# Hybrid encoder on one core: natural token order, banded first dilated group, softmax statistics carried between orders

## The chip, the cores and the metric

The kernel runs on one core of one Trainium2 chip. The metric is device microseconds of one execution; lower is better. The engines are TensorE (PE: matmuls and transposes; its weight loads are listed apart as PEld), VectorE (DVE), ScalarE (ACT), GpSimd (POOL) and SyncE (SP, which here only issues DMAs).

## What is computed

Two layers, 512 tokens, model width 1024, 256 memory tokens. Every layer makes one normalised input, projects it, and runs three branches: differential attention (8 heads, two softmax maps each), dilated attention (3 groups of 4 heads with head width 128), and cross-attention into memory. Each branch is gated by a SiLU path, projected, weighed by sigmoid gates and merged. The change is in the dilated branch:

```python
DIL_GROUPS = ((128, 1), (512, 4), (2048, 16))          # (window, dilation)
for g, (window, dilation) in enumerate(DIL_GROUPS):
    o_g, lse_g = dilated_group(lq[:, :, g], lk[:, :, g], lv[:, :, g], window, dilation, bias_g)
wts = softmax(stack(lses), axis=0)                       # over the groups
o_b = einsum('gbsh,gbshe->bshe', wts, stack(outs))
```

A query of group 0 sees keys at a distance of at most 64 tokens; one of group 1 sees keys of its own class modulo 4 at a distance of at most 256; one of group 2 sees keys of its own class modulo 16. The groups are combined by their softmax denominators, so for a token one softmax over the union of the keys of all three groups gives the same result.

## The kernel before, in words

All large products are made from fp32 values split into a high and a low fp32r part; `mm3` (lines 214 to 217) issues three matmuls for a product. The normalised input lies transposed in `hT_hi` and `hT_lo` [128, 8, 512]. Lines 63 and 64 load and store tokens by class modulo 4: position 128*c + a holds token 4*a + c, so the four chunks of 128 positions are the four classes.

Weights stream in through `load` (line 171, SP queue) in an order written out by hand (`weight_order`), and are split by ScalarE (line 106) and VectorE (line 107) a few units ahead (`prefetch`). `proj_fm` makes 128 features of all tokens (24 matmuls of 512 columns); `proj_tm` makes up to 512 features token-major (four chunks, 96 matmuls as wide as the features).

The attention of a layer is four steps j. In each, `weave` interleaves the tracing of the projections of dilated head j (`dil_proj`) with differential heads 2j and 2j+1 (`diff_att`), and then the projections for the next differential heads (`diff_proj`) with the attention of dilated head j (`dil_att`). The scheduler of the framework then orders each engine's instructions by its own timeline; each engine executes them in that order.

`dil_att` (lines 610 to 660) goes over the four chunks c. For group 0 it makes the scores of 128 queries against all 512 keys (line 628); the bias tile holds minus 1e30 where the key is out of the window, because in class order the window is spread over all four chunks. For groups 1 and 2 it makes 128 x 128 scores within the class, in plain fp32 (line 631). One minimum over both (lines 632 and 635), one exponential over 768 columns (line 638), one reciprocal and one scaling (lines 639 and 640) give the weights of all three groups. They are transposed: four blocks for group 0 (helper, line 506), two for groups 1 and 2 (line 644). V of group 0 is applied with `mm3` to 256 queries at a time (line 650), V of groups 1 and 2 in plain fp32 (line 655), all accumulated in the PSUM tile `d_o`. `dil_proj` makes V of the three groups as one `proj_tm` of 384 features (line 607). `qk_keep` (line 586) copies Q and K of groups 1 and 2 out of PSUM.

`bias_tables` (line 325) makes the bias rows in layer 0 and stores them to DRAM on POOL's queue; `load_bias` (line 361) reads a tile of 7 pieces for a head. `right_sums` (line 256) makes sums of quarters of hT on VectorE (line 259) and stores them to `t_d` (line 281, SP queue) for the matrix products of `pair` in the later merge; it is traced in step j = 1. `diff_norm` (line 557) squares the differential outputs, sums over features with a matmul by ones (lines 565 and 566), and stores the result.

Of the kernel before, what the change touches and what calls it, by code (L numbers as in the profile page):

```python
# [9 lines left out]
F32 = mybir.dt.float32  # L10
F32R = mybir.dt.float32r
# [14 lines left out]
TW = 7 * 255  # L26
# [23 lines left out]
def dil_v_cols(h):  # L50
    return [(g * 128, (g + 1) * 128, LV + g * 512 + h * 128) for g in range(3)]
# [3 lines left out]
def encoder_kernel(ctx: ExitStack, tc: tile.TileContext, x, mem, g_norm, w_in, diff_lambda,  # L55
                   w_mem_kv, g_mem, w_br_diff, w_br_dil, w_br_mem, w_out, rel_bias, g_final,
                   buckets, maskrows, partrows, out):
# [5 lines left out]
    x_v = x[0].rearrange("(a c) d -> c a d", c=4)  # L63
    out_v = out[0].rearrange("(a c) d -> c a d", c=4)
# [23 lines left out]
    tt_d = dr.tile([12, 32, TW], F32, name="tt_d")  # L88
# [21 lines left out]
    def weight_order():  # L110
# [19 lines left out]
        for l in range(DEPTH):  # L130
# [123 lines left out]
    H0, H1 = slice(0, 256), slice(256, 512)  # L254

    def right_sums(pool):

        def acc(out, x, y, op):
            nc.vector.tensor_tensor(out=out, in0=x, in1=y, op=op)

        for k2 in range(2):
            def quarter(kh, ts):
                ks = slice(4 * kh + 2 * k2, 4 * kh + 2 * k2 + 2)
# [3 lines left out]
            t1, t2, t3, t4 = [pool.tile([128, 2, 256], F32, tag="ts", name="t_sum", bufs=4) for _ in range(4)]  # L267
# [12 lines left out]
            for i, t in enumerate((t1, t2, t3, t4)):  # L280
                dma(t_d[i, k2], t)
            yield
# [42 lines left out]
    def bias_tables(pool):  # L325
# [21 lines left out]
        for n0 in range(0, TW, 512):  # L347
            n = min(512, TW - n0)
# [4 lines left out]
            for r in range(4):  # L353
                v = t[r * N_BIAS:r * N_BIAS + 12, 0:n]
                pdma(tt_d[:, r * 8:(r + 1) * 8, n0:n0 + n], v[:, None, :].to_broadcast([12, 8, n]))
                if n0 == 512:
                    v = t[r * N_BIAS + 12:(r + 1) * N_BIAS, 253:508]
                    pdma(t0_d[:, r * 8:(r + 1) * 8, :], v[:, None, :].to_broadcast([8, 8, 255]))

    def load_bias(dst, h):  # L360

        b, nd, w = (tt_d[h], 7, TW) if h < 12 else (t0_d[h - 12], 1, 255)
        for a in range(0, 128, 32):
            dma(dst[a:a + 32], bass.AP(b.tensor, b.offset + 127 - a, [[w - 1, 32], [255, nd], [1, 128]]))
# [91 lines left out]
    def proj_tm(l, key, n, keep):  # L456
# [52 lines left out]
    def diff_att(l, j, P, proj, lam):  # L509
        Q, K, vhi, vlo = proj  # L510
        O = []
        for s in range(2):
            h = 2 * j + s
            bt = P["al"].tile([128, 7, 128], F32, tag="bt", name="f_bias", bufs=2)
# [3 lines left out]
            for half in range(2):  # L518
                whi = P["ae"].tile([128, 4, 256], F32R, tag="x4", name="f_wThi", bufs=4)
                wlo = P["ae"].tile([128, 4, 256], F32R, tag="x4", name="f_wTlo", bufs=4)  # L520
                for c2 in range(2):
# [4 lines left out]
                    for m in range(2):  # L526
                        sp = ps.tile([128, 4, 128], F32, tag="s", name="f_s", bufs=2)
# [4 lines left out]
                        nc.vector.tensor_tensor_reduce(  # L532
                            out=em.rearrange("p (c b) -> p c b", c=4), in0=sp, in1=bt[:, 3 - c:7 - c],
                            op0=ALU.add, op1=ALU.min, scale=-1.0, scalar=3e38, accum_out=stt[:, m:m + 1])
# [22 lines left out]
    def diff_norm(j, P, O):  # L557

        for s, o in enumerate(O):
# [3 lines left out]
            split(sqh, sql, sq)  # L563
            ms = mm([128, S], name="f_ms")
# [19 lines left out]
    def qk_keep(ae, o, scale, name):  # L584
        t = ae.tile([128, S], F32, tag="dqk", name=name, bufs=10)
        nc.scalar.activation(t, o, AF.Copy, scale=scale)
        return t

    def dil_proj(l, h, P):
# [9 lines left out]
        vhi = P["ae"].tile([128, 4, 128], F32R, tag="v1", name="d_vhi", bufs=2)  # L599
        vlo = P["ae"].tile([128, 4, 128], F32R, tag="v1", name="d_vlo", bufs=2)  # L600
        v23 = P["ae"].tile([128, 4, 256], F32, tag="v6", name="d_v23", bufs=2)

        def keep(c, o):
            split(vhi[:, c], vlo[:, c], o[:, 0:128])
            nc.scalar.activation(v23[:, c], o[:, 128:384], AF.Copy)

        yield from proj_tm(l, ("lv", h), 384, keep)
        return Q, K, vhi, vlo, v23

    def dil_att(l, h, P, proj):  # L610
        Q, K, vhi, vlo, v23 = proj
        bt = P["al"].tile([128, 7, 128], F32, tag="bt", name="d_b1", bufs=2)
        load_bias(bt, 8 + h)
        b2 = P["al"].tile([128, 2, 128], F32, tag="b2", name="d_b2", bufs=1)
        load_bias(b2[:, 0:1], 12 + h)
        load_bias(b2[:, 1:2], 16 + h)
        o = ps.tile([128, S], F32, tag="o", name="d_o", bufs=1)
        for half in range(2):
            whi = P["ae"].tile([128, 4, 256], F32R, tag="x4", name="d_wThi", bufs=4)
            wlo = P["ae"].tile([128, 4, 256], F32R, tag="x4", name="d_wTlo", bufs=4)  # L620
            w23 = P["al"].tile([128, 2, 256], F32, tag="w2", name="d_w23", bufs=2)
            for c2 in range(2):
                c = 2 * half + c2
                cs = slice(c * 128, (c + 1) * 128)
                stt = st.tile([128, 8], F32, tag="fst", name="d_st")
                e = P["al"].tile([128, 768], F32, tag="e3", name="d_e", bufs=2)
                sp = ps.tile([128, 4, 128], F32, tag="s", name="d_s1", bufs=2)
                mm3(sp, Q[0][0][:, cs], Q[0][1][:, cs], K[0][0], K[0][1], True, True)
                sp2 = ps.tile([128, 2, 128], F32, tag="s", name="d_s2", bufs=2)
                for g in (1, 2):  # L630
                    nc.tensor.matmul(sp2[:, g - 1], lhsT=Q[g][:, cs], rhs=K[g][:, cs], start=True, stop=True)  # L631
                nc.vector.tensor_tensor_reduce(
                    out=e[:, 0:512].rearrange("p (c b) -> p c b", c=4), in0=sp, in1=bt[:, 3 - c:7 - c],
                    op0=ALU.add, op1=ALU.min, scale=-1.0, scalar=3e38, accum_out=stt[:, 0:1])
                nc.vector.tensor_tensor_reduce(
                    out=e[:, 512:768].rearrange("p (c b) -> p c b", c=2), in0=sp2, in1=b2,
                    op0=ALU.add, op1=ALU.min, scale=-1.0, scalar=stt[:, 0:1], accum_out=stt[:, 1:2])
                nc.scalar.activation(e, e, AF.Exp, scale=-1.0, bias=stt[:, 1:2], accum_out=stt[:, 2:3])
                nc.vector.reciprocal(stt[:, 3:4], stt[:, 2:3])
                nc.vector.tensor_scalar(e, e, stt[:, 3:4], None, op0=ALU.mult)  # L640
                transposed(whi, wlo, [e[:, k * 128:(k + 1) * 128] for k in range(4)], c2 * 128)
                t = ps.tile([128, 2, 128], F32, tag="t", name="w23_ps", bufs=1)
                for k in range(2):
                    nc.tensor.transpose(t[:, k], e[:, 512 + k * 128:640 + k * 128], ident)
                nc.scalar.activation(w23[:, :, c2 * 128:(c2 + 1) * 128], t, AF.Copy)
                if c2 == 0:
                    yield
            oh = o[:, half * 256:(half + 1) * 256]
            for k in range(4):
                mm3(oh, vhi[:, k], vlo[:, k], whi[:, k], wlo[:, k], k == 0, False)  # L650
            for c2 in range(2):
                c = 2 * half + c2
                qs = slice(c2 * 128, (c2 + 1) * 128)
                for g in (1, 2):
                    nc.tensor.matmul(oh[:, qs], lhsT=v23[:, c, (g - 1) * 128:g * 128], rhs=w23[:, g - 1, qs],  # L655
                                     start=False, stop=c2 == 1 and g == 2)
            if half == 0:
                yield
# [162 lines left out]
    for l in range(DEPTH):  # L821
# [29 lines left out]
        P["al"] = al  # L851
        if l > 0:
# [17 lines left out]
        for j in range(4):  # L870
            dp, O = weave((dil_proj(l, j, P), 10), (diff_att(l, j, P, fp, lam), 8))
            if j < 3:
                gens = [(diff_proj(l, j + 1, P), 8), (dil_att(l, j, P, dp), 4)]
                if j == 1:
                    gens.append((right_sums(al), 22))
                fp = weave(*gens)[0]
            else:
                weave((dil_att(l, j, P, dp), 4))
            diff_norm(j, P, O)
# [44 lines left out]
def _shape_constants():  # L924
# [3 lines left out]
    delta = np.arange(-3, 4)[:, None]  # L928
    j = np.arange(-127, 128)[None, :]
    rel = (4 * j + delta).reshape(-1)  # L930
# [13 lines left out]
    return rows, mask.reshape(3, 4 * N_BIAS)  # L944
# [24 lines left out]
```

## Time and profile before

| | us |
|---|---|
| median of 3 runs | 1755.63 |
| lowest to highest | 1754.11 to 1756.03 |
| the profiled execution | 1754.84 |
| its span, first to last instruction | 1753.1 |

Of the span TensorE is busy 98%, weight loads 86%, VectorE 66%, ScalarE 51%, GpSimd 10%. The mean granted TensorE clock is 0.997 of full speed. Matmuls overlap in the records (the duration of one holds the time through the array), so how fast they go is read from the distance between their starts.

### The profile page before, as it was taken

The numbers are of one execution on the slowest core, as the hardware profiler recorded it, in microseconds if no ns is written. First come the engines' busy times: TensorE is split into PE (matmuls) and PEld (weight loads), VectorE is DVE, ScalarE is ACT, GpSimd is POOL, SyncE is SP. The second block draws the span as 40 slices with busy tenths as digits, with TensorE's granted clock in tenths as the row PEclk, the third lists the DMA queues.
The fourth block names the chain that finished last, engine by engine and source line by source line (L and its number), as shares of the span: only waits on it lengthen the run. The fifth ranks groups of instructions, "written<-read, shape, count | busy, mean of one in ns | idle before, by whom it ended". The sixth has DMA issues, their size and how long they took to land.

```text
span 1753.1 us, 25712 instructions
## 1 busy us (share of the span) xinstructions
PE 1724.0 (98%) x9732; PEld 1515.8 (86%) x9732; DVE 1152.4 (66%) x1963; ACT 888.9 (51%) x1516; POOL 174.0 (10%) x141
## 2 busy tenths in 40 slices
PE   7899999999999999999999999999999999999998
PEld 6698889889898889998888998898988888889986
DVE  6766575666766586676476756667657647766663
ACT  6355555545545573343354655455455548533433
POOL 2200000000000033341000000000000100344200
PEclk9999999999999999999999999999999999999999
DMA  9752243332443643332663333324323438333242
GB/s 266 170 135 84 77 119 96 93 89 83 114 132 98 204 145 98 102 108 82 203 190 110 108 95 94 88 82 114 102 78 105 136 90 251 105 97 109 85 151 78
DMA packets 313084, 208.80 MB, mean 119 GB/s; under 512 B 15268, under 2 KB 284580, under 8 KB 312960
## 3 DMA queue, kind: packets, MB, share of 16 engines
q1 hardware_dynamic: 309648, 199.28, 39.0%
q0 software_dynamic: 3312, 7.88, 1.9%
q8 instruction: 76, 1.25, 0.3%
q14 instruction: 48, 0.39, 0.1%
HBM read 182.08 MB, written 25.02 MB: 118 GB/s over the span
## 4 chain that ended last, share of the span: by engine, by line
PE 95%; DMA 2%; DVE 1%; ACT 1%; issue 1%; SPq 0%; ACTq 0%; DVEq 0%
PE mm L215 23%; PE mm L217 23%; PE mm L216 23%; PE s_mm L217 4%; PE s_mm L215 4%; PE s_mm L216 4%; PE wT_ps L506 2%; PE f_s L529 2%; PE f_s L530 2%; DMA w_raw<-in_w_mem_kv 1%; PE f_o L216 1%; PE f_o L215 1%; PE f_o L217 1%; PE d_o L655 1%; PE d_s L631 1%
## 5 line engine op out<-in xcount | busy, mean ns | idle before, releaser
L107 DVE TENSOR_TENSOR w_lo<-w_raw,w_hi 128x1024 fp32r<-128x1024 f32 (+2 forms) x256 | 304.7, 1191 | 218.9 <-PE mm L217 171.6
L106 ACT ACTIVATE w_hi<-w_raw 128x1024 fp32r<-128x1024 f32 (+2 forms) x256 | 250.8, 980 | 389.2 <-PE mm L216 197.4
L215 PE MATMUL mm<-hT_hi,w_hi 128*128 128x512 f32 x1024 | 405.7, 397 | 5.1 <-DVE b_t L352 2.8
L217 PE MATMUL mm<-hT_hi,w_lo 128*128 128x512 f32 x1024 | 403.0, 394 | 0.0
L216 PE MATMUL mm<-hT_lo,w_hi 128*128 128x512 f32 x1024 | 403.0, 394 | 0.0
L215 PEld LDWEIGHTS mm<-hT_hi,w_hi 128*128 128x128 f32 x1024 | 193.2, 189 | 45.6 <-DVE b_t L352 4.5
L217 PEld LDWEIGHTS mm<-hT_hi,w_lo 128*128 128x128 f32 x1024 | 193.0, 188 | 39.9
L216 PEld LDWEIGHTS mm<-hT_lo,w_hi 128*128 128x128 f32 x1024 | 193.4, 189 | 38.1 <-DVE hT_lo L107 0.2
L217 PE MATMUL mm<-w_hi,hT_lo 128*128 128x384 f32 (+2 forms) x640 | 210.0, 330 | 0.0
L215 PE MATMUL mm<-w_hi,hT_hi 128*128 128x384 f32 (+2 forms) x640 | 209.6, 328 | 0.0
L216 PE MATMUL mm<-w_lo,hT_hi 128*128 128x384 f32 (+2 forms) x640 | 208.2, 326 | 0.0
L106 ACT ACTIVATE w_hi<-s_raw 128x1024 fp32r<-128x1024 f32 x80 | 76.1, 952 | 168.7 <-PE mm L216 105.1
L215 PEld LDWEIGHTS mm<-w_hi,hT_hi 128*128 128x128 f32 x640 | 120.9, 189 | 6.0
L216 PEld LDWEIGHTS mm<-w_lo,hT_hi 128*128 128x128 f32 x640 | 120.8, 189 | 6.1
L217 PEld LDWEIGHTS mm<-w_hi,hT_lo 128*128 128x128 f32 x640 | 120.7, 189 | 5.1
L107 DVE TENSOR_TENSOR w_lo<-s_raw,w_hi 128x1024 fp32r<-128x1024 f32 x80 | 99.1, 1239 | 32.8 <-issue 32.8
L535 ACT ACTIVATE f_e<-f_e,f_st 128x512 f32<-128x512 f32 x128 | 92.0, 721 | 49.7 <-DVE f_st L532 49.7
L294 POOL DMA_DIRECT2D t_in<-t_d x16 | 8.9, 562 | 1013.1 <-PE f_o L217 582.2
L215 PE MATMUL mm<-u_hi,w_hi 128*128 128x512 f32 x256 | 101.2, 395 | 0.0
L216 PE MATMUL mm<-u_lo,w_hi 128*128 128x512 f32 x256 | 101.2, 395 | 0.0
L217 PE MATMUL mm<-u_hi,w_lo 128*128 128x512 f32 x256 | 101.1, 395 | 0.0
L532 DVE CUSTOM_DVE_ANT_0 f_e<-f_s,f_bias 128x512 f32<-128x512 f32 x128 | 84.4, 682 | 6.8 <-PE f_s L530 6.7
(248 smaller groups left out, 3365.4 us busy)
## 6 DMA issues: line engine op xcount, KB each, us to landing
w_raw<-in_w_in SPq DMA_DIRECT2D x128, 512.0 KB, 4.0
s_raw<-in_w_in SPq DMA_DIRECT2D x80, 256.0 KB, 3.1
w_raw<-in_w_in SPq DMA_DIRECT2D x96, 128.0 KB, 2.4
w_raw<-in_w_mem_kv SPq DMA_DIRECT2D x16, 512.0 KB, 5.9
w_raw<-in_w_in SPq DMA_DIRECT2D x32, 256.0 KB, 2.9
u_raw<-u_d SPq DMA_DIRECT2D x32, 256.0 KB, 4.8
w_raw<-in_w_br_diff SPq DMA_DIRECT2D x16, 512.0 KB, 4.1
w_raw<-in_w_out SPq DMA_DIRECT2D x16, 512.0 KB, 3.8
```

What stands on the lines that cost most here:

```text
L106: nc.scalar.activation(hi, src, AF.Copy)
L107: nc.vector.tensor_tensor(out=lo, in0=src, in1=f32(hi), op=ALU.subtract)
L215: nc.tensor.matmul(o, lhsT=lh, rhs=rh, start=start, stop=False)
L216: nc.tensor.matmul(o, lhsT=lh, rhs=rl, start=False, stop=False)
L217: nc.tensor.matmul(o, lhsT=ll, rhs=rh, start=False, stop=stop)
L506: nc.tensor.transpose(t[:, i], s, ident)
L529: nc.tensor.matmul(sp, lhsT=qh[:, cs], rhs=K[s, m], start=True, stop=False)
L530: nc.tensor.matmul(sp, lhsT=ql[:, cs], rhs=K[s, m], start=False, stop=True)
L532: nc.vector.tensor_tensor_reduce(out=em.rearrange("p (c b) -> p c b", c=4), in0=sp, in1=bt[:, 3 - c:7 - c], op0=ALU.add, op1=ALU.min, scal ...
L535: nc.scalar.activation(em, em, AF.Exp, scale=-1.0, bias=stt[:, m:m + 1], accum_out=stt[:, 2 + m:3 + m])
L631: nc.tensor.matmul(sp2[:, g - 1], lhsT=Q[g][:, cs], rhs=K[g][:, cs], start=True, stop=True)
L655: nc.tensor.matmul(oh[:, qs], lhsT=v23[:, c, (g - 1) * 128:g * 128], rhs=w23[:, g - 1, qs], start=False, stop=c2 == 1 and g == 2)
```

## The change

Tokens stay in natural order: position is token. So group 0's window is a band, and `dil_att` makes for each block of 128 queries only the scores against its own and the neighbouring blocks (256 columns at the ends, 384 in the middle). On the value side, for each block of keys it transposes the weights of the queries that see it (2 or 3 blocks) and applies V with three matmuls of 256 or 384 columns.

Groups 1 and 2 are still computed by class modulo 4. Their Q and K are brought into class order by the copy in `qk_keep`; their V is projected by class, with every fourth column of hT as weights (`by_class`); and their result is written to every fourth column of `d_o`. V of group 0 is projected for two heads at once, 256 features, with a weight unit of its own (`lv0`); V of groups 1 and 2 is a unit of 256.

Since queries are now in two orders, each has its own minimum, exponential and sum. The new `dil_weights` carries minima and sums from one order into the other with masks and two small fp32 matmuls by a permutation (a new input `orders`, loaded once a layer), takes the common minimum and denominator, and gives one factor per query and order. Scaling by this factor replaces the scaling by the reciprocal.

The bias row is now 1023 + 255 long rather than 7 x 255, made in three matmuls rather than four, and `load_bias` reads one contiguous run per partition; the tile of a dilated head is 384 wide. `right_sums` works in units of 256 columns rather than 512 (40 operations a layer rather than 20), is woven with weight 44 rather than 22, and each operation is bound behind the last softmax operation of `diff_att` traced before it (`mark`, `issue_after`). `diff_norm` is a generator with one yield; at the last step it is woven with `dil_att`. The weave of `dil_proj` has weight 14 rather than 10 at even steps.

```diff
-    x_v = x[0].rearrange("(a c) d -> c a d", c=4)
-    out_v = out[0].rearrange("(a c) d -> c a d", c=4)
+    x_v = x[0].rearrange("(c a) d -> c a d", c=4)
+    out_v = out[0].rearrange("(c a) d -> c a d", c=4)
...
-                yield from tm(l, ("lv", j), 384, dil_v_cols(j))
+                if j % 2 == 0:
+                    yield from tm(l, ("lv0", j), 256, [(0, 256, LV + j * 128)])
+                yield from tm(l, ("lv", j), 256, dil_v_cols(j))
...
+            with tc.issue_after(mark[0].ins):
+                nc.vector.tensor_tensor(out=out, in0=x, in1=y, op=op)
...
-                cs = slice(c * 128, (c + 1) * 128)
+                cs = slice(c, S, 4) if by_class else slice(c * 128, (c + 1) * 128)
...
     def qk_keep(ae, o, scale, name):
-        nc.scalar.activation(t, o, AF.Copy, scale=scale)
+        nc.scalar.activation(t.rearrange("p (c a) -> p a c", c=4), o.rearrange("p (a c) -> p a c", c=4),
+                             AF.Copy, scale=scale)
...
+    def dil_weights(S, P):
+        perm = P["perm"]
+        w = lambda shape, name: P["al"].tile([128] + shape, F32, tag="dw" + name, name="dw_" + name, bufs=1)
+        tt = nc.vector.tensor_tensor
+        o = ps.tile([128, 4, 4, 4], F32, tag="t", name="dw_ps", bufs=1)
+        x, y, R = w([4, 4, 4], "x"), w([4, 4, 4], "y"), w([4, 4], "r")
+        for i in range(2):
+            si, so = slice(2 - 2 * i, 4 - 2 * i), slice(2 * i, 2 * i + 2)
+            own, other = perm[:, i, 128:132], perm[:, 1 - i, 128:132]
+            tt(out=x[:, so], in0=S[:, si, None, :].to_broadcast([128, 2, 4, 4]),
+               in1=own[:, None, :, None].to_broadcast([128, 2, 4, 4]), op=ALU.mult)
+            nc.tensor.matmul(o[:, so], lhsT=perm[:, i, 0:128], rhs=x[:, so], start=True, stop=True)
+            tt(out=y[:, so], in0=o[:, so], in1=other[:, None, None, :].to_broadcast([128, 2, 4, 4]), op=ALU.mult)
+        nc.vector.tensor_reduce(out=R, in_=y, axis=AX.X, op=ALU.add)
...
+        for i in range(4):
+            lo, hi = near(i)
+            n = 128 * (hi - lo + 1)
...
+            qs, ks = slice(128 * i, 128 * i + 128), slice(128 * lo, 128 * lo + n)
+            mm3(sp, q0[0][:, qs], q0[1][:, qs], k0[0][:, ks], k0[1][:, ks], True, True)
...
+        f = dil_weights(S4, P)
...
+                    nc.tensor.matmul(o[:, c:S:4], lhsT=v23[:, c, (g - 1) * 128:g * 128],
+                                     rhs=w23[:, g - 1, c % 2 * 128:c % 2 * 128 + 128], start=c == 0 and g == 1, stop=False)
...
+            oo = o[:, 128 * lo:128 * hi + 128]
+            nc.tensor.matmul(oo, lhsT=vhi[:, i], rhs=whi, start=False, stop=False)
+            nc.tensor.matmul(oo, lhsT=vlo[:, i], rhs=whi, start=False, stop=False)
+            nc.tensor.matmul(oo, lhsT=vhi[:, i], rhs=wlo, start=False, stop=i == 3)
```

## Rows read from the trace of the kernel before

**Rows 1.** The page, busy us of each engine (share of the span), instructions.

```profile
PE 1724.0 (98%) x9732; PEld 1515.8 (86%) x9732; DVE 1152.4 (66%) x1963; ACT 888.9 (51%) x1516; POOL 174.0 (10%) x141
```

**Rows 2.** The page, the chain that ended last: shares of the span.

```profile
PE 95%; DMA 2%; DVE 1%; ACT 1%; issue 1%; SPq 0%; ACTq 0%; DVEq 0%
```

**Rows 3.** What TensorE waited for: us in total, times, longest us.

```profile
PE mm L215 <- DVE b_t L352: 2.8, 1, 2.8
PE f_ms L565 <- ACT f_sqh L106: 2.6, 2, 1.3
```

**Rows 4.** Busy time by stretch: PE, PEld, DVE, ACT, POOL; clock, DMA share, GB/s.

```profile
120.00:480.00 360.00, 359.99 (x2040) 318.64 (x2039) 236.98 (x466) 192.26 (x368) 0.00 (x0) 1.00 0.35 96
```

**Rows 5.** Timeline, 512 columns: start us, us, engine, line; 25 starts apart.

```profile
52.05 0.39 PE L216 MATMUL mm<-hT_lo,w_hi 128*128 128x512 f32 x1
...
57.72 0.39 PE L215 MATMUL mm<-hT_hi,w_hi 128*128 128x512 f32 x1
```

**Rows 6.** Timeline, 256 columns, 34 starts apart.

```profile
229.56 0.28 PE L215 MATMUL mm<-w_hi,hT_hi 128*128 128x256 f32 x1
...
233.63 0.29 PE L216 MATMUL mm<-w_lo,hT_hi 128*128 128x256 f32 x1
```

**Rows 7.** Timeline, 384 columns, 12 starts apart.

```profile
400.21 0.33 PE L215 MATMUL mm<-w_hi,hT_hi 128*128 128x384 f32 x1
...
402.29 0.33 PE L215 MATMUL mm<-w_hi,hT_hi 128*128 128x384 f32 x1
```

**Rows 8.** Timeline: four fp32 passes, four transposes, each followed by 256-column matmuls.

```profile
221.84 0.61 PE L655 MATMUL d_o<-d_w,d_v 128*128 128x128 f32 x4
222.20 0.36 PE L217 MATMUL mm<-w_hi,hT_lo 128*128 128x256 f32 x1
222.40 0.28 PE L215 MATMUL mm<-w_hi,hT_hi 128*128 128x256 f32 x1
...
224.56 0.60 PE L506 MATMUL wT_ps<-ident,d_e 128*128 128x128 f32 x4
224.91 0.37 PE L215 MATMUL mm<-w_hi,hT_hi 128*128 128x256 f32 x1
225.11 0.29 PE L216 MATMUL mm<-w_lo,hT_hi 128*128 128x256 f32 x1
```

**Rows 9.** TensorE's groups by shape: count, busy us, mean ns of one.

```profile
L217 PE MATMUL mm<-w_hi,hT_lo 128*128 128x384 f32 x256 | 87.0, 340 | 0.0
...
L655 PE MATMUL d_o<-d_w,d_v 128*128 128x128 f32 x128 | 19.5, 274 | 0.0
```

**Rows 10.** Tiles d_s and d_e, weight loads: duration ns min/median/max, first to last start.

```profile
L631 PEld LDWEIGHTS d_s<-d_k,d_q x128: 187/190/193, 190.6 to 1414.0; 128*128 128x128 f32 x128
...
L506 PEld LDWEIGHTS wT_ps<-ident,d_e x128: 137/141/147, 198.5 to 1437.4; 128*128 128x128 f32 x128
```

**Rows 11.** Timeline of the start: SP's queue, ScalarE, TensorE; idle before and its releaser.

```profile
51.73 10.32 SPq L281 DMA_DIRECT2D t_d<-t_sum  x4
...
68.15 1.06 ACT L106 ACTIVATE w_hi<-w_raw 128x1024 fp32r<-128x1024 f32 x1 [6.83 <-DMA w_raw<-in_w_in]
...
71.29 0.80 PE L215 MATMUL mm<-hT_hi,w_hi 128*128 128x512 f32 x1 [2.79 <-DVE b_t L352]
```

**Rows 12.** Busy time by stretch at the start (columns as in rows 4).

```profile
66.00:72.00 6.00, 1.97 (x12) 1.45 (x11) 5.96 (x9) 2.83 (x3) 0.47 (x1) 0.93 0.89 277
72.00:76.00 4.00, 4.00 (x14) 3.17 (x13) 3.96 (x13) 2.14 (x9) 3.55 (x8) 0.68 0.84 169
```

**Rows 13.** Groups of VectorE and ScalarE by shape: count, busy us, mean ns of one.

```profile
L107 DVE TENSOR_TENSOR w_lo<-w_raw,w_hi 128x768 fp32r<-128x768 f32 x32 | 30.6, 958 | 49.9 <-PE mm L217 49.8
L259 DVE TENSOR_TENSOR t_sum<-t_sum,hT_lo 128x512 f32<-128x512 f32 x24 | 15.8, 683 | 0.1
L242 DVE TENSOR_TENSOR mgate<-s_mm,mgate 128x256 f32<-128x256 f32 x140 | 56.3, 418 | 40.4 <-PE s_mm L217 40.3
...
L586 ACT ACTIVATE d_q<-mm 128x512 f32<-128x512 f32 x16 | 9.3, 580 | 0.0
```

More of the change, by code (lines that the diff above doesn't have):

```diff
@@ L25 @@
 NEG = -1e30
-TW = 7 * 255
+TW = 1023 + 255
 QSCALE = 128.0 ** -0.5
@@ L50, in dil_v_cols, with near @@
 def dil_v_cols(h):
-    return [(g * 128, (g + 1) * 128, LV + g * 512 + h * 128) for g in range(3)]
+    return [((g - 1) * 128, g * 128, LV + g * 512 + h * 128) for g in (1, 2)]
+def near(i):
+    return max(i - 1, 0), min(i + 1, 3)
 @with_exitstack
@@ L603, in keep @@
         def keep(c, o):
[L604 to L608, printed above, removed]
+            nc.scalar.activation(v23[:, c], o, AF.Copy)
+        yield from proj_tm(l, ("lv", h), 256, keep, True)
+        hs = slice(h % 2 * 128, h % 2 * 128 + 128)
+        return Q, K, V0[0][:, :, hs], V0[1][:, :, hs], v23
+    V0 = []
+    def dil_weights(S, P):
[12 more added lines that the diff above has]
+        nc.vector.tensor_reduce(out=R, in_=y, axis=AX.X, op=ALU.add)
+        n, z = w([2, 4], "n"), w([2, 2, 4], "z")
+        tt(out=n, in0=S[:, 0:4:2], in1=R[:, 0:4:2], op=ALU.min)
+        for i, t in enumerate((S, R)):
+            tt(out=z[:, i], in0=n, in1=t[:, 0:4:2], op=ALU.subtract)
+        nc.scalar.activation(z, z, AF.Exp)
+        d = w([2, 4], "d")
+        tt(out=d, in0=S[:, 1:4:2], in1=z[:, 0], op=ALU.mult)
+        tt(out=z[:, 1], in0=R[:, 1:4:2], in1=z[:, 1], op=ALU.mult)
+        tt(out=d, in0=d, in1=z[:, 1], op=ALU.add)
+        nc.vector.reciprocal(d, d)
+        f = P["al"].tile([128, 2, 4], F32, tag="dwf", name="dw_f", bufs=2)
+        tt(out=f, in0=z[:, 0], in1=d, op=ALU.mult)
+        return f
@@ L617, in dil_att @@
+        f = dil_weights(S4, P)
         o = ps.tile([128, S], F32, tag="o", name="d_o", bufs=1)
-        for half in range(2):
-            whi = P["ae"].tile([128, 4, 256], F32R, tag="x4", name="d_wThi", bufs=4)
-            wlo = P["ae"].tile([128, 4, 256], F32R, tag="x4", name="d_wTlo", bufs=4)
+        for c2 in range(2):
             w23 = P["al"].tile([128, 2, 256], F32, tag="w2", name="d_w23", bufs=2)
[L622 to L629, printed above, removed]
-                for g in (1, 2):
[L631 to L657, printed above, removed]
@@ new lines, in dil_att @@
+        yield
+        for i in range(4):
+            e = seg[i][0]
+            nc.vector.tensor_scalar(e, e, f[:, 0, i:i + 1], None, op0=ALU.mult)
+        for i in range(4):
+            lo, hi = near(i)
+            nb = hi - lo + 1
+            whi = P["ae"].tile([128, 3, 128], F32R, tag="x4", name="d_wThi", bufs=4)[:, 0:nb]
+            wlo = P["ae"].tile([128, 3, 128], F32R, tag="x4", name="d_wTlo", bufs=4)[:, 0:nb]
+            t = ps.tile([128, 3, 128], F32, tag="t", name="wT_ps", bufs=1)[:, 0:nb]
+            for j in range(lo, hi + 1):
+                e, _, first = seg[j]
+                nc.tensor.transpose(t[:, j - lo], e[:, 128 * (i - first):128 * (i - first) + 128], ident)
+            split(whi, wlo, t)
+            oo = o[:, 128 * lo:128 * hi + 128]
+            nc.tensor.matmul(oo, lhsT=vhi[:, i], rhs=whi, start=False, stop=False)
+            nc.tensor.matmul(oo, lhsT=vlo[:, i], rhs=whi, start=False, stop=False)
+            nc.tensor.matmul(oo, lhsT=vhi[:, i], rhs=wlo, start=False, stop=i == 3)
+            if i == 1:
@@ L874, in encoder_kernel @@
                 if j == 1:
-                    gens.append((right_sums(al), 22))
+                    gens.append((right_sums(al), 44))
                 fp = weave(*gens)[0]
-            else:
-                weave((dil_att(l, j, P, dp), 4))
-            diff_norm(j, P, O)
+                for _ in diff_norm(j, P, O):
+                    pass
+            else:
+                weave((dil_att(l, j, P, dp), 4), (diff_norm(j, P, O), 4))
         close(al_c)
@@ L943, in _shape_constants @@
         mask[g, :, 8 + 4 * g:12 + 4 * g] = NEG
-    return rows, mask.reshape(3, 4 * N_BIAS)
+    i = np.arange(128)
+    orders = np.zeros((128, 2, 132), np.float32)
+    to_block = i[:, None] % 32 == i[None, :] // 4
+    orders[:, 0, :128], orders[:, 1, :128] = to_block, to_block.T
+    orders[i, 0, 128 + i // 32] = 1.0
+    orders[i, 1, 128 + i % 4] = 1.0
+    return rows, mask.reshape(3, 4 * N_BIAS), orders
 def kernel(**inputs):
@@ L954 @@
     import ml_dtypes
-    rows, mask = _shape_constants()
+    rows, mask, orders = _shape_constants()
     rows = np.concatenate([rows] * 3).astype(ml_dtypes.bfloat16)
@@ L958 @@
     feed = {k: inputs[k] for k in _INS}
-    feed["buckets"], feed["maskrows"], feed["partrows"] = rows, mask, part
+    feed["buckets"], feed["maskrows"], feed["partrows"], feed["orders"] = rows, mask, part, orders
     for name, a in feed.items():
```

97 lines of the change are left out of this document (65 added, 32 removed).

## The prediction, made before the changed kernel was run

> **What bounds the kernel now.** I read the page's busy shares first: TensorE is busy 1724.0 of 1753.1 us, VectorE 66%, ScalarE 51% [rows 1]. A busy TensorE may still crawl, so the chain that ended last comes next: 95% of it is TensorE [rows 2]. The list of what TensorE waited for holds little beyond the first 50 us: 2.8 us on the bias-table copy and 2.6 us on diff_norm's split [rows 3]. In the 360 us from 120 to 480 it is busy 359.99 us [rows 4]. So the kernel is a queue of matmuls, and an edit is worth what it does to the start-to-start spacing of matmuls. Durations on the matmul rows overlap, so the spacing is read from a timeline: 512 columns, 25 steps in 5.67 us, 0.227 us [rows 5]; 256 columns, 34 steps in 4.07 us, 0.120 us [rows 6]; 384 columns, 12 steps in 2.08 us, 0.173 us [rows 7]. Four plain fp32 passes of 128 columns (a plain fp32 product is two instructions, so the 64 of line 655 are counted as 128 [rows 9]) and one 256-column matmul take 0.56 us, so a pass is 0.11 us; a transpose, read the same way, is 0.108 us [rows 8].
>
> **The change, part by part.** *Group 0, which leaves the full score matrix.* Per head, QK is now 4 x 3 matmuls of 512 columns, 12 x 0.227 = 2.72 us, and becomes 6 of 256 and 6 of 384: 6 x 0.120 + 6 x 0.173 = 1.76 us. PV is now 24 matmuls of 256 columns, 2.88 us, and becomes the same 1.76 us. Transposes fall from 16 to 10: 6 x 0.108 = 0.65 us. Together 0.96 + 1.12 + 0.65 = 2.73 us, for 8 heads (4 in each of 2 layers) 21.8 us, all on TensorE and so all on the path.
>
> *The V projection.* Before, 384 matmuls of 384 columns in a layer (x256 for each of the three lines of mm3 over both layers, one of them in [rows 9]): 384 x 0.173 = 66.4 us. After, group 0 of two heads together makes 2 x 96 matmuls of 256 columns and groups 1 and 2 make 4 x 96: 576 x 0.120 = 69.1 us. That adds 2.7 us a layer, 5.4 us.
>
> *Carrying the statistics.* dil_weights adds 2 plain fp32 products of 32 columns per head, 4 passes. No row shows 32 columns: between a quarter of 0.11 us (if only columns count) and 0.11 us (if the load of 128 weights counts), 0.11 to 0.44 us a head. I take the upper end, because the passes of 128 and the transposes already sit at one value: 8 x 0.44 = 3.5 us (0.9 at least).
>
> *Strided operands.* V of groups 1 and 2 now takes as weights every fourth column of hT (a step of 16 bytes): 2 layers x 4 heads x 96 = 768 weight loads. And the 128 passes of line 655 now write every fourth element of d_o. No row of before has a strided matmul operand. The bounds: free, or half speed. No spacing is under 0.108 us, so I take that for the load. A load of twice 0.108 us no longer hides behind 0.120 us and costs 768 x (0.216 - 0.120) = 74 us; 128 passes at twice 0.11 us cost 14 us. A gain is excluded, since the loads are as many and as wide. I take both at nothing. The nearest rows for that: the load of a transpose is recorded at 0.137 to 0.147 us, that of an ordinary fp32 matmul at 0.187 to 0.193 us, both 128 x 128 [rows 10]; contiguous columns can thus be fetched about 0.05 us faster than ordinary loads ask for, and a fetch that is slower by that much would still fit.
>
> The Trainium skill speaks against this. "SBUF — State Buffer", Specifications (TRN2), says that a 16-byte line wants at least two hits for full bandwidth and that each crossing to a new line pays; no run so far shows it here, and by it the sum would end near 1812 us. "PSUM — Partial Sum Buffer", Specifications (TRN2), says that any non-contiguous access pattern slows matmuls significantly; by that the sum would end near 1752 us.
>
> *The start.* In layer 0 the scheduler pulled right_sums forward: t_sum operations sit on VectorE between 47 and 75 us, and their stores to t_d sit on SP's queue: four issues of line 281 hold that queue for 10.32 us from 51.73, and the weight loads of line 171 stand behind them. ScalarE then waits 6.83 us for a weight, and TensorE 2.79 us for the copy into b_t, which VectorE has queued behind that weight [rows 11]. From 66 to 72 us it is busy 1.97 of 6 us, and from 72 to 76 the granted clock is 0.68, a mix of 1.2 and 2.4 GHz [rows 12]. The new issue_after holds these sums behind a softmax operation of diff_att in the second head pair, so VectorE and SP are free at 60 us; there is also one bias matmul, copy and set of POOL stores less. The gap is worth 4.0 us and the low clock after it 4 x 0.32 = 1.3 us. The next in line is the transfer of the weights themselves (DMA share 0.89 and 0.84 there [rows 12]), so I take 4 us, between 0 and 5.3.
>
> *diff_norm at the last head.* It is now woven with dil_att; the waits of 2.6 us in both layers [rows 3] can go, or stay because the wait is for ScalarE. I take 1 us (0 to 2.6).
>
> *Edits that cost TensorE nothing, and their cover.* Weights of 256 columns instead of 384: VectorE splits go from 32 x 0.958 us to 48 of 512 columns in all, at 0.683 as in line 259, 2.1 us more [rows 13]. right_sums go from 40 operations of 0.683 us to 80 of 256 columns at 0.42 (the duration of mgate's adds [rows 13]): 27 to 34 us. The copies of line 586 write in class order; at worst they double, 32 x 0.58 = 18.6 us on ScalarE [rows 13]. Per head, dil_weights adds about 13 small VectorE operations at 0.16 to 0.29 us, and the narrower reductions and splits give that back. VectorE is idle 600 us, ScalarE 864 us, so this lies beside matmuls. The new waits: TensorE's two small products and then the transposes wait for VectorE and ScalarE in turn, and everything behind them in TensorE's order waits too. In heads 0 to 2 the next diff_proj (33 us of matmuls) stands between, and the present chain of softmax, reciprocal, scaling and transpose makes no entry in the waits [rows 3]. So 0; without the cover (last head) each of the three points where TensorE takes over (two products, first transposes) costs at most the 1.3 us that was the longest wait on diff_norm's split [rows 3], 4 us a layer. Behind t_d's stores on SP stand weight loads, as before, now in the second pair where three weights are ahead. Bias loads get longer runs and, for group 0, fewer bytes; the load of orders (two) sits among several hundred: nothing.
>
> *The sum.* -21.8 + 5.4 + 3.5 - 4 - 1 = -17.9 us on the profiled execution's own 1754.84 us (its span plus 1.74 us around it): 1737 us. That execution is 0.8 us under the median of 1755.63, which makes 1738 us for a median. Its own range is 1732 (0.9 for 3.5 on the statistics, 5.3 and 2.6 for the gains of 4 and 1) to 1746 (no cover for the last heads).
>
> **The rivals.** *A: the strided weight loads are slow, and it is slower.* For it: spacing 0.120 us leaves only 0.012 us above the 0.108 of the smallest pass, so any slower load shows one for one. Against it: the faster load of the transposes. It turns the sign when a load takes 0.120 + 17.9/768 = 0.143 us, a third more than 0.108; at twice the load the time is 1738 + 74 = 1812 us. The line rule of the Trainium skill's "SBUF — State Buffer", Specifications (TRN2), is this mechanism.
>
> *B: the strided writes into d_o are slow.* 128 passes at twice their time: 1752 us, about no change. For it: a plain fp32 pass is already the slowest per column in the trace. Against: at 0.11 us for 128 columns the output comes only every 0.86 ns, against 0.44 ns at 512 columns in 0.227 us, so there is slack.
>
> *C: the chain of the statistics stalls TensorE.* If all 8 heads pay 4 us, the time is 1738 + 32 = 1770 us; if only the last head of each layer does, 1746 us. Against it stand the waits of before.
>
> *D: the start gives nothing back,* because the transfers bound it: 1743 us, inside the forecast's own range.
>
> **How the numbers follow.** The forecast with D has 0.53, A 0.30 (any slowdown of the loads that ends above 1759 us), B 0.10, C 0.07. Faster by over 0.2% means under 1752.1 us, slower means over 1759.1; 0.2% is about what a measurement of this kernel can tell from no change. Faster: 0.53, half of B and 0.03 of C (its milder form), 0.61. Same: the other half of B and 0.02 of C, 0.07. Slower: A and 0.02 of C, 0.32. The likeliest case's own range is 1732 to 1746 us. To hold 8 in 10 the range must reach into A: 1730 to 1813 us.
>
> **What would show it.** Right: matmuls d_s and d_o at 256 and 384 columns with spacings 0.120 and 0.173 us; the by-class V matmuls at 0.120 us and their loads recorded near 0.19 us; line 655's successors still at 0.11 us a pass; no t_sum before 120 us and no low clock near 72 us; TensorE busy all but some 25 us. Wrong: a spacing of 0.15 us or more in the by-class projection (A); passes into d_o at 0.2 us (B); entries in TensorE's waits for dil_weights' tiles (C).

## The result: slower, by the price of one operand

The changed kernel takes 1835.06 us (median of 4 runs, 1834.03 to 1838.59) against 1755.83 us of the kernel before on the same chip: a ratio of 1.0456, 95% interval 1.0443 to 1.0468, 79 us slower. The forecast was 1738 us with a range of 1730 to 1813: both miss, and the sign too. It was rival A, the strided weight loads, and it costs more than the price that A was given.

The page of after, first busy us and instructions of each engine, then the shares of the chain that ended last (beside [rows 1] and [rows 2]):

```profile
PE 1795.2 (98%) x10003; PEld 1593.3 (87%) x10003; DVE 1143.6 (62%) x2106; ACT 882.8 (48%) x1562; POOL 164.1 (9%) x133
...
PE 93%; DMA 3%; DVE 2%; ACT 1%; issue 0%; SPq 0%; DVEq 0%; ACTq 0%
```

TensorE is busy 98% of the span, as before, and still 93% of the chain that ended last. Its busy time rose by 71 us, though there is less arithmetic to do. So the question is which matmuls became slower, and again only spacing tells. Timeline of after (start us, us, engine, line), the by-class projection of V:

```profile
176.65 0.40 PE L223 MATMUL mm<-w_lo,hT_hi 128*128 128x256 f32 x1
176.88 0.40 PE L224 MATMUL mm<-w_hi,hT_lo 128*128 128x256 f32 x1
...
178.75 0.40 PE L223 MATMUL mm<-w_lo,hT_hi 128*128 128x256 f32 x1
178.98 0.40 PE L224 MATMUL mm<-w_hi,hT_lo 128*128 128x256 f32 x1
```

From 176.65 to 178.98 us the whole timeline has 10 steps, 0.233 us each, where [rows 6] has 0.120 for the same 256 columns. The weight-load track of the same stretch shows why:

```profile
176.75 0.33 PEld L224 LDWEIGHTS mm<-w_hi,hT_lo 128*128 128x128 f32 x1
176.98 0.33 PEld L222 LDWEIGHTS mm<-w_hi,hT_hi 128*128 128x128 f32 x1
```

Each load is recorded at 0.33 us instead of 0.19, and the loads follow one another at 0.23 us, as the matmuls do. 768 x (0.233 - 0.120) = 87 us.

What else was foretold can be read in the same trace. The strided writes into d_o cost nothing: eight passes and then a transpose, in the timeline of after:

```profile
239.83 1.05 PE L706 MATMUL d_o<-d_w,d_v 128*128 128x128 f32 x8
240.72 0.60 PE L702 MATMUL w_ps<-ident,d_e 128*128 128x128 f32 x4
```

0.89 us for 8 passes, 0.111 each, the price of contiguous ones in [rows 8]. The start is repaired (busy time by stretch: PE, PEld, DVE, ACT, POOL; clock, DMA share, GB/s):

```profile
66.00:72.00 6.00, 6.00 (x31) 4.99 (x31) 4.22 (x12) 3.36 (x9) 4.45 (x8) 1.00 0.83 153
72.00:76.00 4.00, 4.00 (x21) 3.36 (x20) 2.14 (x6) 1.51 (x5) 0.00 (x0) 1.00 0.43 87
```

TensorE is busy throughout at a granted clock of 1.00, the 2.4 GHz level, where [rows 12] have 1.97 us of 6 and then a clock of 0.68. And TensorE has new waits (us in total, times, longest; the entries for the first 50 us are left out):

```profile
PE f_s L539 <- DVE f_st L542: 5.1, 6, 1.1
PE d_s L222 <- DVE d_st L685: 3.0, 2, 1.5
...
PE f_ms L576 <- ACT f_sqh L111: 2.4, 2, 1.2
PE f_ms L577 <- DVE f_sql L112: 1.9, 2, 0.9
```

[rows 3] had the first of the two f_ms kinds alone (the wait for f_sqh), 2.6 us. The new ones lie in two places: at the step from one head pair to the next (f_s), and at the last head of each layer (d_s, and the wait of f_ms for f_sql).

### The profile page after: what moved, and what is told of

The parts are those of the page before. It is cut to its first block, busy times and chain, and to the rows that moved or that the text cites. A ratio compares the mean times of both kernels' runs of the same rounds, so it can differ in the third digit from the quotient of the medians.

```text
span 1832.4 us, 26443 instructions
## 1 busy us (share of the span) xinstructions
PE 1795.2 (98%) x10003; PEld 1593.3 (87%) x10003; DVE 1143.6 (62%) x2106; ACT 882.8 (48%) x1562; POOL 164.1 (9%) x133
## 4 chain that ended last, share of the span: by engine, by line
PE 93%; DMA 3%; DVE 2%; ACT 1%; issue 0%; SPq 0%; DVEq 0%; ACTq 0%
PE mm L222 23%; PE mm L223 23%; PE mm L224 23%; PE s_mm L224 4%; PE s_mm L222 4%; PE s_mm L223 4%; DMA w_raw<-in_w_in 2%; PE f_s L539 2%; PE f_s L540 1%; PE wT_ps L516 1%; DMA w_raw<-in_w_mem_kv 1%; PE f_o L223 1%; PE f_o L224 1%; PE f_o L222 1%; DVE w_lo L112 1%; PE d_s L684 1%
## 5 line engine op out<-in xcount | busy, mean ns | idle before, releaser
L112 DVE TENSOR_TENSOR w_lo<-w_raw,w_hi 128x1024 fp32r<-128x1024 f32 (+1 forms) x272 | 305.2, 1124 | 320.6 <-PE mm L224 177.4
L111 ACT ACTIVATE w_hi<-w_raw 128x1024 fp32r<-128x1024 f32 (+1 forms) x272 | 253.1, 933 | 472.9 <-PE mm L223 232.3
L223 PE MATMUL mm<-w_lo,hT_hi 128*128 128x256 f32 (+1 forms) x768 | 259.3, 339 | 0.0
L224 PE MATMUL mm<-w_hi,hT_lo 128*128 128x256 f32 (+1 forms) x768 | 257.5, 338 | 0.0
L222 PE MATMUL mm<-w_hi,hT_hi 128*128 128x256 f32 (+1 forms) x768 | 256.0, 339 | 0.0
L223 PEld LDWEIGHTS mm<-w_lo,hT_hi 128*128 128x128 f32 x768 | 181.3, 236 | 5.9
L224 PEld LDWEIGHTS mm<-w_hi,hT_lo 128*128 128x128 f32 x768 | 181.0, 236 | 5.6
L222 PEld LDWEIGHTS mm<-w_hi,hT_hi 128*128 128x128 f32 x768 | 179.4, 236 | 6.2
L112 DVE TENSOR_TENSOR w_lo<-s_raw,w_hi 128x1024 fp32r<-128x1024 f32 x80 | 99.3, 1242 | 44.3 <-issue 29.3
L545 ACT ACTIVATE f_e<-f_e,f_st 128x512 f32<-128x512 f32 x128 | 91.6, 717 | 29.3 <-DVE f_st L542 29.2
```

The source lines that it names most:

```text
L111: nc.scalar.activation(hi, src, AF.Copy)
L112: nc.vector.tensor_tensor(out=lo, in0=src, in1=f32(hi), op=ALU.subtract)
L222: nc.tensor.matmul(o, lhsT=lh, rhs=rh, start=start, stop=False)
L223: nc.tensor.matmul(o, lhsT=lh, rhs=rl, start=False, stop=False)
L224: nc.tensor.matmul(o, lhsT=ll, rhs=rh, start=False, stop=stop)
L545: nc.scalar.activation(em, em, AF.Exp, scale=-1.0, bias=stt[:, m:m + 1], accum_out=stt[:, 2 + m:3 + m])
```

## The experiments

**The loads alone** (e1 from here on). Theory: the stride in the weight operand is the whole loss. Rival: part of it comes from elsewhere in the new by-class work (the copies in class order, the order of work).

```
-  cs = slice(c, S, 4) if by_class else slice(c * 128, (c + 1) * 128)
+  cs = slice(c * 128, (c + 1) * 128)
```

> The changed kernel, with the V projection of groups 1 and 2 taking 128 neighbouring columns of hT as weights in place of every fourth (so V of these groups belongs to the wrong tokens; nothing else differs, and every engine's instructions stand in the same order). Theory A, the strided weight loads: 768 matmuls go back from a spacing of 0.233 us to 0.120 us, 87 us less, so 1835 becomes about 1748 us, a little faster than before. Rival C, the new chain of statistics and the weave stall TensorE: no change, about 1835 us.

Measured 1749.67 us (6 runs), ratio to before 0.9969 (0.9955 to 0.9983). TensorE executes the same instructions in the same order as in after, and the profiled spans differ by 1832.4 - 1745.4 = 87.0 us, for 768 x 0.113 = 86.8. Compared matmul by matmul the agreement is a little less close: 85.4 us are steps of 0.233 for 0.120; 2.9 us lie at the last heads, where the granted clock in after is 0.96 (550 to 595 and 1450 to 1495 us) and in e1 1.00 (515 to 560 and 1372 to 1417 us); and 1.4 us go the other way before 80 us. Its weight loads by line, for by-class V and every other projection that takes hT as weights (count, busy us, mean ns; after has 236 ns in this row):

```profile
L223 PEld LDWEIGHTS mm<-w_lo,hT_hi 128*128 128x128 f32 x768 | 146.2, 190 | 6.3
```

So the change without the strided loads (and so with V of the wrong tokens) is faster by 0.3%, and with them slower by 4.6%. That settles A. It also shows that the forecast, its loads apart, was 12 us too low; that is taken up below.

**How the price depends on the step.** The four k2 units of the projection (tiles a, b, c, d) take their weights at steps of 1, 2, 3 and 4 elements. Theory: a price by how many elements share 16 bytes. Rival: a price by how many share 8.

```
-  cs = slice(c, S, 4) if by_class else ...
+  cs = slice(0, 128 * (k2 + 1), k2 + 1) if by_class else ...
```

> The changed kernel, with the four weight units of the by-class V projection loaded at steps of 1, 2, 3 and 4 columns (4, 8, 12, 16 bytes; V of groups 1 and 2 belongs to the wrong tokens; the weights of the four units are named a, b, c, d). 192 matmuls at each step. If only a step to a new 16-byte line with every column is slow: steps 1 and 2 at 0.120 us, step 3 between, step 4 at 0.233 us, about 1748 + 22 + 15 = 1785 us. If every column that is not beside the last one is slow: steps 2, 3 and 4 all at 0.233 us, about 1748 + 65 = 1813 us.

Measured 1780.88 us (one run). The loads by tile (count, busy us, mean ns):

```profile
L223 PEld LDWEIGHTS mm<-d_hi,hT_hi 128*128 128x128 f32 x64 | 21.0, 329 | 0.0
...
L223 PEld LDWEIGHTS mm<-c_hi,hT_hi 128*128 128x128 f32 x64 | 16.6, 260 | 0.1
...
L223 PEld LDWEIGHTS mm<-b_hi,hT_hi 128*128 128x128 f32 x64 | 12.6, 196 | 0.3
...
L223 PEld LDWEIGHTS mm<-a_hi,hT_hi 128*128 128x128 f32 x64 | 12.2, 191 | 0.2
```

and the spacing at step 3 and at step 2 in the timeline:

```profile
184.18 0.34 PE L224 MATMUL mm<-c_lo,hT_hi 128*128 128x256 f32 x1
...
186.10 0.34 PE L223 MATMUL mm<-c_hi,hT_hi 128*128 128x256 f32 x1
...
287.03 0.28 PE L224 MATMUL mm<-b_lo,hT_hi 128*128 128x256 f32 x1
...
288.95 0.28 PE L225 MATMUL mm<-b_hi,hT_lo 128*128 128x256 f32 x1
```

11 steps in 1.92 us are 0.174 us at step 3; 16 steps in 1.92 us are 0.120 at step 2, nothing over contiguous; step 4 keeps 0.233 (the median of its spacings in this trace). The Trainium skill's "SBUF — State Buffer", Specifications (TRN2), says that a 16-byte line wants at least two hits; the trace agrees: at 8 bytes two elements share such a line and the load is free, at 12 only some do, at 16 none. The sizes fit too: at 12 bytes 128 elements lie on 96 such lines, three quarters of the 128 at 16 bytes, and 0.174 is three quarters of 0.233. What these four steps can't tell apart is a price by lines and a price by the bytes passed over; they would part beyond 16 bytes, and no run has such a step.

**Additive, or hidden behind a wider matmul?** The kernel before, its V projection of 384 columns with every fourth column as weights.

> The kernel before, with the one edit that its 384-column V projection takes every fourth column of hT as weights (all three V then belong to the wrong tokens; the order of instructions on every engine is that of before). 768 strided loads, each in front of a matmul of 384 columns instead of 256. If a strided load takes 0.233 us and runs beside the matmul in front of it, the spacing is 0.233 instead of 0.173 us: 46 us, 1802 us. If striding adds 0.113 us to each matmul however wide it is: 87 us, 1843 us. If the strided loads are not the cause: 1756 us.

Measured 1801.87 us (one run). Timeline:

```profile
179.97 0.40 PE L215 MATMUL mm<-w_hi,hT_hi 128*128 128x384 f32 x1
...
181.14 0.40 PE L217 MATMUL mm<-w_hi,hT_lo 128*128 128x384 f32 x1
```

5 steps in 1.17 us: 0.234 us, the same as under 256 columns, where an added 0.113 would have made 0.286. The load lies beside the matmul in front and sets the pace alone; it isn't added to it.

**The start alone.** The kernel before with the sums held back, nothing else (`mark` holds the last softmax reduction of `diff_att` traced before; the lines that set it are left out):

```
-            nc.vector.tensor_tensor(out=out, in0=x, in1=y, op=op)
+            with tc.issue_after(mark[0].ins):
+                nc.vector.tensor_tensor(out=out, in0=x, in1=y, op=op)
...
```

> The kernel before with one part of the change alone: the sums of right_sums are held behind a softmax reduction of the second head pair. The theory that the early sums and their stores on SP's queue are what TensorE waits for at 66 to 76 us: the kernel loses 7 us as read from the trace of after (3.0 us instead of 10.2 us lost between 40 and 80 us), 1748.5 us. If part of that came from the shorter bias tables (one matmul, copy and set of stores less), 1751 to 1753 us; if all, 1755.6 us.

Measured 1750.59 us against 1756.25, ratio 0.9965 (0.9952 to 0.9977): 5.7 us, most of the 7. In its trace TensorE loses 5.7 us from 40 to 80 us where before loses 10.2 (lost is what starts of matmuls are further apart than their shape needs). The first t_sum now runs at 289.1 us, and the stretch is whole:

```profile
66.00:72.00 6.00, 6.00 (x34) 5.02 (x32) 5.78 (x15) 5.06 (x13) 3.36 (x6) 1.00 0.47 96
72.00:76.00 4.00, 4.00 (x22) 3.33 (x20) 2.65 (x6) 1.54 (x2) 3.36 (x7) 1.00 0.90 191
```

So the early sums were the cause of the gap. This one part of the change, put into the old kernel, gives as much as all of it gives in e1, and beats both the kernel before and after.

**The last head.** In e1 TensorE stalls where before it did not. Is it the weave of diff_norm? The last step is traced as before:

```
-  weave((dil_att(l, j, P, dp), 4), (diff_norm(j, P, O), 4))
+  weave((dil_att(l, j, P, dp), 4))
+  for _ in diff_norm(j, P, O):
+      pass
```

> The kernel after with contiguous weight loads (V of groups 1 and 2 is made for the wrong tokens, as in e1_plain_loads), and in the last step of a layer diff_norm is traced behind dil_att again, as in the kernel before, and no longer woven with it. In e1 TensorE loses 5.9 us at 520 to 560 us and 7.0 us at 1360 to 1400 us, where the kernel before lost 2.2 and 2.7 us. If weaving diff_norm (its 3.35 us reciprocal on VectorE stands among the reductions of the scores) is the cause, these 8 us come back and the time is 1742 us. If the last head stalls for want of other matmuls to run meanwhile, wherever diff_norm stands, it stays at 1749 us (1748 to 1751).

Measured 1751.05 us, ratio 0.9967 (0.9955 to 0.9979): no different from e1. The scheduler puts f_ms and the reciprocal into the same places whichever way they are traced (the last two f_ms matmuls of layer 0 start at 532.8 and 537.5 us in e1 and at 533.6 and 538.3 here, all of it 0.8 us later), so the weave neither helps nor harms.

Is it want of other matmuls (e9)? The first three gate projections of the merge (72 matmuls) are traced beside the last head:

```
+  def first_gates():
+      for i in U_ORDER[:3]:
+          early.append(gate(l, U_COLS[i]))
+          yield
...
-  weave((dil_att(l, j, P, dp), 4), (diff_norm(j, P, O), 4))
+  weave((dil_att(l, j, P, dp), 4), (first_gates(), 4), (diff_norm(j, P, O), 4))
```

> e1_plain_loads (after with contiguous weight loads; V of groups 1 and 2 is made for the wrong tokens) with the first three gate projections of the merge traced woven with the last dilated head. e1 lost 5.9 and 7.0 us in the last steps and the kernel before 2.2 and 2.7. If want of other matmuls is the cause, it is at before's level: 1750 - 8 = 1742 us, which is what the forecast's sum gives with the true start. If the VectorE chain sets the pace: 1750 us.

Measured 1772.16 us, 22 us slower than e1. The matmuls did go between the scores, and were missing later. From the waits of TensorE and its timeline in this run:

```profile
PE mm L222 <- DVE gate L315: 20.1, 2, 10.2
...
593.85 0.28 PE L725 MATMUL d_o<-d_wTlo,d_v0hi 128*128 128x256 f32 x1
604.29 0.79 PE L222 MATMUL mm<-hT_hi,w_hi 128*128 128x512 f32 x1 [10.16 <-DVE gate L315]
```

and what stood in front of that gate operation, on SP's queue and on VectorE:

```profile
595.15 0.34 SPq L321 DMA_DIRECT2D u_d<-o_sb  x1
...
596.02 2.59 SPq L781 DMA_DIRECT2D u_raw<-u_d  x5
...
600.62 0.69 DVE L789 TENSOR_TENSOR u_raw<-u_raw,gate 128x512 f32<-128x512 f32 x1 [5.34 <-DMA u_raw<-u_d]
```

VectorE waits for u_raw, whose load is issued only at 596.02 us. On SP's queue it stands behind the store of the last head's result (u_d<-o_sb), and that store waits 5.1 us for ScalarE's copy of the result, which comes after the last matmul of the head (593.85 us). The gate operations that would free PSUM banks stand behind the u_raw operation on VectorE. In e1 the last head ends some 20 us earlier (the store is issued at 575.38 us), and TensorE still had gate projections to do in this time: it is busy 60.00 of the 60 us from 560 on, against 49.84 here, at a granted clock of 0.91. And even with other matmuls in between, the last step is not whole: the waits of d_s are gone, but TensorE is busy 41.57 of 45 us (515 to 560) where e1 has 40.15, and two waits of 2.6 us for f_sqh remain. So want of matmuls is one part of the stall at most, and taking them from the next stage costs more there than it gives here. What else sets the pace of the last step stays open.

**Other ways to V by class.** First (e4), by feature (48 matmuls of 512 columns a head, contiguous loads), copied into class order and transposed on TensorE:

```
-  yield from proj_tm(l, ("lv", h), 256, keep, True)
...
+  o = proj_fm(l, LV + g * 512 + h * 128)
...
+  nc.scalar.activation(t.rearrange("p (c a) -> p a c", c=4), o.rearrange("p (a c) -> p a c", c=4), AF.Copy)
...
+  nc.tensor.transpose(o[:, c], t[:, c * 128:(c + 1) * 128], ident)
...
```

> The changed kernel without strided loads, whole: V of groups 1 and 2 is projected feature-major like Q and K (48 matmuls of 512 columns per head, 10.9 us, instead of 96 of 256), copied out in class order and transposed on TensorE (8 per head, 0.9 us). If the strided loads are the cause, TensorE needs 11.8 us per head in place of 22.4, 85 us less in all: about 1750 us, faster than before by 0.3%. If the rest of the change is itself no gain: 1756 us or more.

Measured 1763.11 us (5 runs), ratio 1.0043 (1.0029 to 1.0057). The loads are cured, 72 us against after, but 13 us are missing. They lie in the last steps (a window of e4, the same window of e1, then a wait of e4 over the whole run):

```profile
515.00:560.00 45.00, 39.32 (x199) 33.11 (x198) 25.81 (x59) 21.39 (x44) 3.77 (x7) 0.85 0.31 100
...
515.00:560.00 45.00, 40.15 (x230) 34.60 (x230) 29.03 (x60) 23.16 (x48) 0.54 (x1) 1.00 0.38 115
...
PE wT_ps L517 <- DVE f_wTlo L112: 5.8, 4, 2.6
```

TensorE idles 5.7 of 45 us and the granted clock of the stretch is 0.85: some of it ran at 1.2 GHz after the idling. e1 idles 4.9 us in the same window, only 0.8 us less, and keeps 1.00. So most of the missing time is the low clock that followed, not the idling itself: 0.15 x 45 = 6.8 us a layer, an estimate. Among the six executions of e1 the time goes with the mean granted clock in the same way: 1746.82 us at 0.999, 1753.82 at 0.992.

Two attempts at that stall. The share of dil_proj in the weave lowered from 14 and 10 to 12 and 8:

> e4_v_by_feature (V of groups 1 and 2 by feature, then transposed; the whole computation) with one change: in the weave of dil_proj and diff_att the share of dil_proj falls from 14 and 10 to 12 and 8 pieces, because its last two pieces are only eight transposes and no projection. In e4 TensorE lost 13.3 and 13.6 us in the last step of the layers: its matmuls of the projection were used up while diff_att still had its last blocks to do. If that is the cause, most of the 27 us less the 13 that e1 shows there comes back: 1750 us (1747 to 1752). If it isn't, the time stays at 1763 us.

Measured 1763.86 us: no effect, so the theory fell; it was the other of its two cases. And the first gates traced early:

> e4_v_by_feature (V of groups 1 and 2 by feature; the whole computation) with one change of order: the first three gate projections of the merge, 72 matmuls of 512 columns, are traced woven with the attention of the last dilated head, so that TensorE has them to run while VectorE and ScalarE do the softmaxes. e4 lost 13.3 and 13.6 us in the last steps. If what is missing there is other matmuls, each falls to about 3 us: 1763 - 21 = 1742 us. If the chain of VectorE (the 3.35 us reciprocal in front of reductions and splits) sets the pace whatever TensorE does meanwhile, or the matmuls are then missing behind, it stays at 1763 us.

Measured 1781.81 us, neither of its two times: the matmuls are missing behind, as it had considered, but at the price of the same 10 us hole as in e9, 20.4 us in both layers together.

Second, two heads at once, so that one strided load serves 512 columns (the share of dil_proj in the weave of the odd steps, which have less to project, goes from 10 to 6):

> The whole computation. V of groups 1 and 2 is again projected by class with every fourth column of hT as weights, but for two heads at once: 384 matmuls of 512 columns where after has 768 of 256, so half as many strided loads. With it five gate projections of the merge woven with the last dilated head. If the load takes 0.233 us and lies beside the matmul in front (0.227 us), the spacing of these matmuls is 0.233 us and the projection costs 384 x 0.233 = 89.5 us where contiguous loads with 256 columns cost 768 x 0.120 = 92.2: 1740 us if the odd steps, which now have less projection to run beside attention, don't stall, up to 1752 if they lose 3 us each. If the strided load adds its extra 0.113 us to every matmul whatever its width, 384 x 0.107 = 41 us more: 1781 us.

Measured 1792.06 us, far from 1740 and past the bound of 1752. But the part that the run was for is plain in its timeline:

```profile
175.00 0.39 PE L222 MATMUL mm<-w_hi,hT_hi 128*128 128x512 f32 x1
175.23 0.40 PE L223 MATMUL mm<-w_lo,hT_hi 128*128 128x512 f32 x1
175.47 0.39 PE L224 MATMUL mm<-w_hi,hT_lo 128*128 128x512 f32 x1
```

0.235 us a step here, 0.237 in the median of the run, against 0.227 contiguous [rows 5]: behind 512 columns the strided load all but disappears. The loss is TensorE's idling and the low clock after it: the two holes behind the early gates (16.8 us together; from 560 to 620 us TensorE is busy 47.11 of 60 us at a granted clock of 0.83) and the odd steps, left with less projection beside attention (7.7 and 7.8 us lost in the stretches of 40 us from 320 and from 1200 us, against 2.1 and 0.3 in e1). Whether an arrangement of the order exists that keeps TensorE busy with this V projection was not settled.

## Why the prediction was wrong, point by point

**The step that failed** is "Strided operands ... I take both at nothing". For the writes into d_o it held: 0.111 us a pass. For the weight loads the row it rested on was no neighbour. [rows 10] shows that transposes' loads are recorded 0.05 us shorter than ordinary ones, and the prediction concluded that a fetch slower by as much would still fit. Both of those loads read contiguous columns; the row says nothing of a step. Measured, the strided load sets a spacing of 0.233 us. The condition that A named, a load over 0.143 us, was the right test. Only its upper bound was too low: twice the smallest spacing seen (0.216) is no bound, and 0.233 gives 87 us for 74. That is 13 of the 22 us by which the result passes the range's end at 1813; the rest is the stalls below.

**Group 0, V and the statistics were right.** I price the matmuls of before and e1 by shape, at 0.227, 0.173, 0.119 and 0.109 us for 512, 384, 256 and 128 columns: without the statistics' passes the sum falls by 17.8 us, where the forecast's terms make -21.8 + 5.4 = -16.4. The V projection is +4.2 and not +5.4 (0.119 for 0.120 on 576 matmuls a layer). The two passes of each small product begin 0.03 and 0.11 us ahead of what follows, and the matmul behind them takes 0.20 us to the next for 0.12: 0.22 us a product, 3.6 us for 16 where other matmuls stand beside them. That is the 3.5 that the forecast took, its upper bound.

**The start gave 6 us, not 4.** From 40 to 80 us TensorE loses 10.2 us before and 4.0 in e1; the run of the start alone gives 4.5 in this stretch of its trace and 5.7 as a median. The forecast stopped at its fear of the transfers behind, and its bound of 5.3 counted only the gap and the low clock from 66 to 76 us.

**diff_norm at the last head** was to give 1 us and C's milder form to cost 4 us a layer. C's form came: the last steps lose 7.2 us in each layer of e1 (515 to 560 and 1360 to 1400 us) against 2.2 and 2.7 before, 4.7 us a layer more. (The 5.9 us of the expectations is the first of them counted from 520 us on.) In the first of these windows TensorE is busy 43.65 of 45 us before and 40.15 in e1. The points are only partly those that it named: the scores that wait for a reduction (1.5 us a layer), f_ms, and the two products.

**What no rival had** is the loss at the step from one head pair to the next. There the forecast had looked at the chain of the statistics alone, which 33 us of diff_proj do cover; the stall comes when diff_proj is used up. TensorE's timeline in e1:

```profile
231.88 0.40 PE L577 MATMUL f_ms<-f_sql,ones 128*128 128x512 f32 x1
233.21 0.50 PE L539 MATMUL f_s<-f_k,f_qh 128*128 128x512 f32 x1 [0.93 <-DVE f_st L542]
```

and VectorE's of the same time:

```profile
231.00 1.21 DVE L112 TENSOR_TENSOR w_lo<-w_raw,w_hi 128x1024 fp32r<-128x1024 f32 x1
232.13 0.42 DVE L112 TENSOR_TENSOR f_vlo<-mm,f_vhi 128x256 fp32r<-128x256 f32 x1
232.46 0.68 DVE L542 CUSTOM_DVE_ANT_0 f_e<-f_s,f_bias 128x512 f32<-128x512 f32 x1
```

The next pair's scores wait for VectorE, which has the splits of a weight and of f_vlo in front of the reduction that frees the bank. Six times, 5.3 us in e1. All stretches but the start and the last steps lose 29.3 us in e1 against 22.0 before, 7.3 more: these waits, 2.7 us for the 12 small products outside the last steps, and 0.7 us less elsewhere.

The account of e1 against before by these, in the profiled executions: -17.8 (shapes) - 6.2 (start) + 9.4 (last steps) + 7.3 (all the rest) = -7.3 us, where the spans differ by -7.7 (1745.4 for 1753.1). Adding 87 gives after. So without the loads the sum of -17.9 would still have been 10 us too hopeful. Shapes, start and small products gave a little more than it had; the last steps, which it had as a gain of 1 us and only in rival C as a loss, and the steps between head pairs, which it had nowhere, took more than that back.

**The covers of the other edits held.** VectorE is busy 1143.6 us for 1152.4, ScalarE 882.8 for 888.9. The copies in class order did what was bounded, nearly double the 0.58 us of [rows 13], and off the path:

```profile
L598 ACT ACTIVATE d_q<-mm 128x512 f32<-128x512 f32 x16 | 17.3, 1080 | 0.0
```

## What to carry to other kernels

Where weight loads run just under the matmuls in spacing, the step of the stationary operand is part of the matmul's price: at a step of two fp32 elements it was free, at three 0.054 and at four 0.113 us over a 256-column matmul, and hardly anything behind 512 columns. Take the price of an operand pattern from a row that has that pattern, and when none has, let the size of the possible loss (here 768 loads against a gain of 18 us) and not the nearest contiguous row decide the likeliest case. And matmuls moved forward to fill a hole are missing where they were: look at what they covered there before counting the gain.

## What the runs showed of the hardware

- The weight load of 128 x 128 fp32r at steps of 4, 8, 12 and 16 bytes: recorded 191, 196, 260 and 329 ns, matmul spacing at 256 columns 0.120, 0.120, 0.174 and 0.233 us (e2).
- That load, at 16 bytes, lies beside the matmul in front: 0.233 us under 256 columns (after), 0.234 under 384 (e3), 0.235 under 512 (e10).
- TensorE's clock after short idling: in e4 it idles 5.7 of 45 us at a last head and the granted clock of the stretch is 0.85; in e1 it idles 4.9 and keeps 1.00.
- PSUM writes with a step of 16 bytes cost a plain fp32 matmul of 128 columns nothing, 0.111 us a pass. The Trainium skill's "PSUM — Partial Sum Buffer", Specifications (TRN2), says that any non-contiguous pattern slows matmuls significantly; in this kernel the measurement differs.
- A ScalarE copy of 128 x 512 that writes in hops of 512 bytes took 1.08 us, for 0.58 in [rows 13].
